# An fp32 encoder kernel: one of four remainders of the up projection's weights by a negated copy and an adding transfer

## The chip, the cores and the metric

The kernel runs on one core of one Trainium2 chip. The metric is device time in microseconds of one launch. A core has five engines that run their own instruction queues in order and meet at semaphores: TensorE (PE in the profile, with its weight loads as PEld), VectorE (DVE), ScalarE (ACT), GpSimd (POOL) and SyncE (SP). Transfers are issued from a queue of SP, ACT or POOL and carried out by 16 DMA engines.

## The reference

Two layers of a bidirectional encoder on 256 tokens of width 2048, in float32:

```python
for l in range(DEPTH):                       # 2
    h = rms_norm(x, ln1_g[l])
    proj = h @ w_in[l]                       # 2048 x 4608
    ...                                      # two groups of 8 heads: neighbourhood attention, windowed GQA
    x = x + o @ w_out[l]
    h2 = rms_norm(x, ln2_g[l])
    u = depthwise_conv(h2 @ w_up[l], conv_w[l], conv_b[l])     # 2048 x 11264, width 3 over positions
    gate, up = u[..., :D_FF], u[..., D_FF:]                    # D_FF = 5632
    x = x + (jax.nn.silu(gate) * up) @ w_down[l]
```

## The kernel before

**Products in parts.** The large products are computed in a reduced float32 format (F32R). To keep the accuracy, each factor is split in two parts: a high part, which is a copy rounded to F32R, and a remainder, the value minus the high part. Three products (high x high, high x remainder, remainder x high) are summed. `split` does it: ScalarE writes the high part (line 112), VectorE subtracts (line 113). For weights the tiles are `raw` (as loaded), `whi` and `wlo`.

**Quanta and half blocks.** All weights stream through the core once, in quanta of 1 MB (`raw`, 128 x 2048 floats, 3 buffers), loaded by SP's queue (line 742). A quantum is split and used in two halves of 128 x 1024 (three parts for the kind "seven"). A list `steps` of (quantum, half) sets the order; at step s the program first calls `split_w(s + SPLIT_AHEAD)` with SPLIT_AHEAD = 4, and then the products of step s. When the last half of a quantum has been split, the load of the quantum three further on is issued into its buffer. `whi` and `wlo` have five buffers each, so the split for step s + 4 waits until PE has finished step s - 1.

**The stages of a layer.** Input projection with attention around it, output projection, and then the feed-forward part. There, an *up block* is one 128-wide slice of gate and up columns: two quanta, four half blocks. After each block ScalarE evacuates PSUM (line 546), VectorE adds and scales (547, 548), POOL fills the halo of the convolution with two tiny copies (550, 551), ScalarE and VectorE do the convolution and the gate (556 to 562). The 44 up blocks come in runs of 9, 8, 8, 8 and 8, and three more that alternate with sevens. Between the runs stand quanta of the down projection: "plain", "seven" (one level of a scheme with seven products, whose raw weights VectorE combines first, lines 748 to 750) and "down".

**What sets the order.** The program is written in the order of `steps`; a scheduler places each instruction on its engine's queue by a simulated timeline and by priorities: a block under `tc.high_priority(offset=AHEAD_PRIO)` goes 40 places ahead. Tiles named `v_a` and `v_b` are the values of attention's two groups, 128 x 1024 floats each; in the feed-forward part nothing uses them.

Of the kernel before, what the change touches and what calls it, by code (L numbers as in the profile page):

```python
# [11 lines left out]
F32 = mybir.dt.float32  # L12
F32R = mybir.dt.float32r
I32 = mybir.dt.int32
AF = mybir.ActivationFunctionType
ALU = mybir.AluOpType
AX = mybir.AxisListType

P = 128
L = 2  # L20
T = 256
TT = T // P
# [18 lines left out]
NB = 4  # L41
# [8 lines left out]
AHEAD_PRIO = 40  # L50
# [3 lines left out]
WARM = 14  # L54

SPARE = 3 * (("qT", 3),)


@with_exitstack
def encoder_kernel(  # L60
# [5 lines left out]
    nc = tc.nc  # L66
    const = ctx.enter_context(tc.tile_pool(name="const", bufs=1))
    wp = ctx.enter_context(tc.tile_pool(name="wp", bufs=2))
    act = ctx.enter_context(tc.tile_pool(name="act", bufs=1))
# [27 lines left out]
    def mm(ps, lhsT, rhs, start, stop):  # L97
        nc.tensor.matmul(ps, lhsT, rhs, start=start, stop=stop, skip_group_check=True)  # L98

    def rsqrt(ps, inv_n, dst, tag):  # L100

        v = work.tile(list(dst.shape), F32, name="v_" + tag, bufs=1)
        nc.vector.tensor_scalar(v, ps, inv_n, EPS, op0=ALU.mult, op1=ALU.add)
        e = power[:, 0:math.prod(dst.shape[1:])]
        if len(dst.shape) == 3:
            e = e.rearrange("p (t h) -> p t h", t=TT)
        nc.gpsimd.tensor_tensor(dst, v, e, op=ALU.pow)
# [19 lines left out]
    st = {}  # L127
# [6 lines left out]
    def square_x(nb):  # L134
        if nb == 0:

            st["ss"] = act.tile([P, TT, NB + 24], F32, name="ss_x")[:, :, 0:NB]
        for tt in range(TT):
            sq = work.tile([P, TT, T], F32, name="prob", bufs=2)
            nc.scalar.activation(sq.rearrange("p t n -> p (t n)"), x[:, tt, nb * 512:(nb + 1) * 512], AF.Square,  # L140
                                 accum_out=st["ss"][:, tt, nb:nb + 1])
# [26 lines left out]
    def stat_o(grp):  # L168
        ps = psum.tile([P, TT], F32, name="pv", bufs=1)
        for tt in range(TT):  # L170
            mm(ps[:, tt:tt + 1], acc_o[grp][:, tt * P:(tt + 1) * P], ones[:, 0:1], True, True)
        st["ro"] = act.tile([P, TT], F32, name="ro", bufs=2)
        rsqrt(ps, 1.0 / (NH * HD), st["ro"], "c2")


# [229 lines left out]
    quanta = []  # L405
# [113 lines left out]
    def middle(l, f):  # L519

        name, bufs = "mid", MIDS
        if f >= NF - CHUNKS[-1]:
            k = count[l] = count.get(l, 0) + 1
            if k > MIDS:
                name, bufs = SPARE[k - MIDS - 1]
        return act.tile([P, 2, T], F32R, name=name, bufs=bufs)

    def q_up(l, f, u):
        def body(q, half, hi, lo):
            if u == 0 and half == 0:  # L530
                cur["up"] = psum.tile([P, 2, 2, T], F32, name="mm", bufs=2)
            ps = cur["up"]
            hv, lv = (w.rearrange("p (k j n) -> p k j n", k=4, j=2) for w in (hi, lo))
            for j in range(2):
                for kk in range(4):
                    k = 8 * u + 4 * half + kk
                    two(ps[:, j], hv[:, kk, j], lv[:, kk, j], xs[k], k == 0, k == KD - 1)
            if u == 1 and half == 1:
                glu(l, f, ps)
        return body  # L540
# [28 lines left out]
    ms, ss = {}, {}  # L569
# [15 lines left out]
    def q_seven(l, c, i):  # L585

        f = sum(CHUNKS[:c]) + 2 * i
        p = f // 2
        a, b = slice(0, P), slice(P, T)

        def body(q, part, hi, lo):
            if i == 0 and part == 0:
                t = psum.tile([P, 2, 512], F32, name="mm", bufs=2)
                ps = {1: t[:, 0], 6: t[:, 1]}
                for n, name, k in ((5, "S", 2), (7, "S", 2), (3, "tr", 1), (4, "pv", 1)):
                    ps[n] = psum.tile([P, 512], F32, name=name, bufs=k)
                cur["seven"] = ps
            ps = cur["seven"]
            hv, lv = (w.rearrange("p (k n) -> p k n", k=2) for w in (hi, lo))
            todo = (((3, ss[p, 3]), (1, gs[f][:, :, a])),  # L600
                    ((7, ss[p, 2]), (5, ss[p, 0])),
                    ((4, gs[f + 1][:, :, b]), (6, ss[p, 1])))[part]
            for j, (n, x2) in enumerate(todo):
                for x_part, w in ((0, hv), (1, hv), (0, lv)):
                    mm(ps[n], x2[:, x_part], w[:, j], i == 0 and x_part == 0 and w is hv,
                       i == PAIRS - 1 and w is lv)
            if i == PAIRS - 1 and part == 2:
                with tc.high_priority(offset=AHEAD_PRIO):
                    add_seven(ps)
        return body  # L610
# [89 lines left out]
    for l in range(L):  # L700
# [8 lines left out]
        for c, nf in enumerate(CHUNKS):  # L709
            up = lambda f: [(a["w_up"][l, f, u], q_up(l, f, u), "up") for u in range(2)]  # L710
            down = lambda nb, g: [(a["w_down"][l, sum(CHUNKS[:c]) // FG + g, nb], q_down(l, c, nb, g), "")]
            seven = lambda i: [(a["w_seven"][l, c, i], q_seven(l, c, i), "seven")]
# [17 lines left out]
                    quanta += down(nb, g)  # L730


    steps = [(q, h) for q in range(len(quanta)) for h in range(3 if quanta[q][2] == "seven" else 2)]
    raw, hl, left, loads, highs = {}, {}, {}, {}, {}

# [8 lines left out]
    def split_seven(w, part, hi, lo):  # L744

        hv, lv = (t.rearrange("p (k n) -> p k n", k=2) for t in (hi, lo))
        if part == 1:
            nc.vector.tensor_sub(w[:, 1:3], w[:, 1:3], w[:, 2:4])
            nc.vector.tensor_add(w[:, 3], w[:, 3], w[:, 1])
            nc.vector.tensor_sub(w[:, 0], w[:, 3], w[:, 0])  # L750
        return split(hv, lv, (w[:, 1::2], w[:, 1:3], w[:, 0::3])[part])

    def split_w(s, parts=1):
        if s < len(steps):
            q, half = steps[s]
            kind = quanta[q][2]
            o = UP_AT if kind == "up" else 0
            hl[s] = tuple(wp.tile([P, 1024 + 64], F32R, name=t, bufs=SPLIT_AHEAD + 1)[:, o:o + 1024]
                          for t in ("whi", "wlo"))
            with tc.high_priority(offset=AHEAD_PRIO if s >= KD // 2 else 0):  # L760
                if kind == "seven":
                    highs[s] = split_seven(raw[q].rearrange("p (k n) -> p k n", k=4), half, *hl[s])
                else:
                    m = 1024 // parts
                    for j in range(parts):
                        highs[s] = split(*(t[:, j * m:(j + 1) * m] for t in hl[s]),
                                         raw[q][:, half * 1024 + j * m:half * 1024 + (j + 1) * m])
            left[q] -= 1
            if left[q] == 0:
                del raw[q]  # L770
                load(q + LOAD_AHEAD)
# [15 lines left out]
    def first_x(i):  # L787
        for j in range(2):
            prep_x(0, 0, 2 * i + j, xT[i][:, j, :])
# [64 lines left out]
    for s, (q, half) in enumerate(steps):  # L854
        if s + SPLIT_AHEAD < KD // 2:
            first_x(s + SPLIT_AHEAD)
        split_w(s + SPLIT_AHEAD)
        quanta[q][1](q, half, *hl.pop(s))
        for f, args in side.pop((q, half), []):
            f(*args)  # L860
# [101 lines left out]
```

## Time and profile before

| what | value |
|---|---|
| time, median of 3 runs | 2090.1 us (2090.08 to 2090.17) |
| profiled execution: span, first to last instruction | 2088.2 us |
| granted TensorE clock | 1.000 |
| DVE, ACT, POOL busy | 82%, 59%, 8% of the span |
| DMA engines | mean 196 GB/s; 405 MB on SP's queue |
| splits of weights | 797 on ACT (1.057 us mean), 797 on DVE (1.221 us mean) |
| loads of 1 MB | 4.9 us from issue to landing (median) |

The profiled execution's own time is its span; the runs' median is 1.9 us above it, which lies around the span. In a group's row stand line, engine, operation, output <- input, shapes, count, then busy time and mean ns of one, then the idle time of the engine just before them and what ended most of it. In the list of waits stand engine, line, what ended the wait, then total us, times and the longest. A timeline row begins with start and duration in us.

### The profile page before, as it was taken

The page shows a single profiled execution, that of the slowest core. Times are in us where ns is not written, and L with a number is a line of the kernel's source. Part 1 is how long each engine was busy: PE and PEld are TensorE (multiplying, and loading weights), DVE is VectorE, ACT ScalarE, POOL GpSimd, SP SyncE. Part 2 cuts the span into 40 slices and gives each one's busy share as a digit, 9 for nine tenths or more (in the row PEclk, how much of TensorE's full clock was granted, in tenths as well). Part 3 has the DMA queues.
Part 4 walks back from the last instruction along what each step waited for, and adds up shares of the span by engine and source line. Part 5 has one row for each costly group of instructions (what it writes and reads, how often), then busy time and mean ns, then how long its engine had stood idle before and what let it go on. Part 6 is the DMA issues. An engine that isn't in the chain of part 4 may idle for free.

```text
span 2088.2 us, 29195 instructions
## 1 busy us (share of the span) xinstructions
PE 2082.8 (100%) x10816; PEld 1788.6 (86%) x10816; DVE 1719.4 (82%) x2604; ACT 1222.1 (59%) x1817; POOL 175.4 (8%) x237
## 2 busy tenths in 40 slices
PE   9999999999999999999999999999999999999999
PEld 8888888888888888888888888888888888888887
DVE  7786657898898988989757766578989989899896
ACT  7566556555555556556555665565656565555553
POOL 0011100100101001011000111001001010010100
PEclk9999999999999999999999999999999999999999
DMA  9544555556565564656655445555565655656554
GB/s 353 196 144 168 176 179 173 194 200 207 179 242 184 209 211 165 240 194 210 208 182 182 162 166 171 169 180 195 208 202 175 235 195 204 204 187 232 184 200 161
DMA packets 62143, 408.41 MB, mean 196 GB/s; under 512 B 7344, under 2 KB 9904, under 8 KB 13744
## 3 DMA queue, kind: packets, MB, share of 16 engines
q1 hardware_dynamic: 61280, 405.46, 56.4%
q8 instruction: 85, 1.39, 0.3%
q10 hardware_dynamic: 720, 1.08, 0.2%
q14 instruction: 58, 0.48, 0.1%
HBM read 404.42 MB, written 2.10 MB: 195 GB/s over the span
## 4 chain that ended last, share of the span: by engine, by line
PE 100%; ACT 0%; DVE 0%; issue 0%
PE mm L98 90%; PE S L98 4%; PE pv L98 3%; PE tr L98 2%; PE tr L373 1%; PE tr L307 1%; PE S L149 1%; ACT v_a L263 0%; ACT mid L115 0%; DVE x L689 0%; DVE ones L90 0%; DVE halfpi L94 0%; DVE power L92 0%
## 5 line engine op out<-in xcount | busy, mean ns | idle before, releaser
L112 ACT ACTIVATE whi<-raw 128x1024 fp32r<-128x1024 f32 (+1 forms) x797 | 830.8, 1057 | 684.3 <-PE mm L98 403.0
L113 DVE TENSOR_TENSOR wlo<-raw,whi 128x1024 fp32r<-128x1024 f32 (+1 forms) x797 | 964.8, 1221 | 271.9 <-ACT whi L112 234.6
L98 PE MATMUL mm<-xs,whi 128*128 128x512 f32 x2816 | 977.0, 390 | 0.0
L98 PE MATMUL mm<-xs,wlo 128*128 128x256 f32 x2816 | 794.1, 282 | 0.0
L98 PEld LDWEIGHTS mm<-xs,whi 128*128 128x128 f32 x2816 | 528.3, 188 | 110.5
L98 PEld LDWEIGHTS mm<-xs,wlo 128*128 128x128 f32 x2816 | 532.2, 189 | 1.1
L98 PE MATMUL mm<-whi,mid 128*128 128x512 f32 x1412 | 369.4, 391 | 0.4 <-ACT v_a L263 0.4
L98 PEld LDWEIGHTS mm<-whi,mid 128*128 128x128 f32 x1412 | 262.6, 188 | 54.5 <-ACT v_a L263 0.9
L98 PE MATMUL mm<-whi,xs 128*128 128x512 f32 x1152 | 294.7, 393 | 0.1
L98 PEld LDWEIGHTS mm<-whi,xs 128*128 128x128 f32 x1152 | 212.7, 188 | 42.6 <-ACT whi L112 0.8
L98 PE MATMUL mm<-wlo,mid 128*128 128x512 f32 x706 | 201.8, 391 | 0.0
L98 PE MATMUL mm<-wlo,xs 128*128 128x512 f32 x576 | 158.8, 392 | 0.0
L98 PEld LDWEIGHTS mm<-wlo,mid 128*128 128x128 f32 x706 | 132.2, 188 | 27.2
L558 DVE SCALAR_TENSOR_TENSOR pT<-halo,conv,pT 128x256 f32<-128x256 f32 x352 | 148.3, 480 | 0.9
L550 POOL COPY halo<-halo 128x6 f32<-128x6 f32 x88 | 40.6, 461 | 1233.6 <-DVE halo L548 1233.6
L98 PEld LDWEIGHTS mm<-wlo,xs 128*128 128x128 f32 x576 | 107.0, 188 | 21.4
L556 ACT ACTIVATE pT<-halo,conv 128x256 f32<-128x256 f32 x176 | 95.1, 588 | 5.8 <-DVE halo L548 5.7
L551 POOL COPY halo<-halo 128x6 f32<-128x6 f32 x88 | 76.0, 864 | 0.2 <-POOL halo L550 0.2
L548 DVE TENSOR_TENSOR halo<-prob,acc_b 128x512 f32<-128x512 f32 x88 | 60.7, 690 | 1.9
L547 DVE TENSOR_TENSOR prob<-prob,mm 128x512 f32<-128x512 f32 x88 | 60.0, 681 | 0.0
L546 ACT ACTIVATE prob<-mm 128x512 f32<-128x512 f32 x88 | 51.4, 584 | 7.1 <-PE mm L98 7.1
L560 ACT ACTIVATE prob<-pT 128x256 f32<-128x256 f32 x88 | 35.6, 404 | 30.3 <-DVE pT L558 30.3
(180 smaller groups left out, 1479.8 us busy)
## 6 DMA issues: line engine op xcount, KB each, us to landing
raw<-in_w_up SPq DMA_DIRECT2D x176, 1024.0 KB, 4.9
raw<-in_w_in SPq DMA_DIRECT2D x71, 1024.0 KB, 4.9
raw<-in_w_down SPq DMA_DIRECT2D x48, 1024.0 KB, 4.9
raw<-in_w_seven SPq DMA_DIRECT2D x40, 1024.0 KB, 4.9
raw<-in_w_out SPq DMA_DIRECT2D x32, 1024.0 KB, 4.8
raw<-in_w_plain SPq DMA_DIRECT2D x10, 1024.0 KB, 4.8
bias<-in_bias SPq DMA_DIRECT2D x16, 160.0 KB, 3.1
x<-in_x SPq DMA_DIRECT2D x4, 512.0 KB, 10.0
```

The costliest lines, as they stand in the source:

```text
L98: nc.tensor.matmul(ps, lhsT, rhs, start=start, stop=stop, skip_group_check=True)
L112: high = nc.scalar.activation(hi, src, AF.Copy)
L113: nc.vector.tensor_sub(lo, src, hi.bitcast(F32))
L149: nc.tensor.transpose(ps[:, j, tt * P:(tt + 1) * P], x[:, tt, (k + j) * P:(k + j + 1) * P], ident)
L546: nc.scalar.activation(t, ps[:, :, 0], AF.Copy)
L547: nc.vector.tensor_add(t, t, ps[:, :, 1])
L548: nc.vector.tensor_mul(ux[:, :, r:r + T], t, st["r2"][:, None, :].to_broadcast([P, 2, T]))
L550: nc.gpsimd.tensor_copy(ux[:, :, 1:r], ux[:, :, T:T + r - 1])
L551: nc.gpsimd.tensor_copy(ux[:, :, T + r:T + 2 * r - 1], ux[:, :, r + 1:2 * r])
L556: nc.scalar.activation(y[:, j, :], ux[:, j, r:r + T], AF.Identity, scale=w1, bias=b)
L558: nc.vector.scalar_tensor_tensor(y[:, j, :], ux[:, j, o:o + T], w, y[:, j, :], op0=ALU.mult, op1=ALU.add)
L560: nc.scalar.activation(t[:, 0, :], y[:, 0, :], AF.Silu)
```

## The change

For the last of the four half blocks of every up block (88 in all) the remainder is no longer a subtraction on VectorE. ScalarE writes the negated, rounded copy of `raw` into a tile, and a transfer issued on POOL's queue adds `raw` to it. This starts seven steps ahead instead of four, while the high part of that half is still copied at four. The remainders lie in `v_a` and `v_b` in turn. Two other tiles change their size by some bytes.

```diff
+EARLY = 7
...
-            st["ss"] = act.tile([P, TT, NB + 24], F32, name="ss_x")[:, :, 0:NB]
+            st["ss"] = act.tile([P, TT, NB + 20], F32, name="ss_x")[:, :, 0:NB]
...
-        st["ro"] = act.tile([P, TT], F32, name="ro", bufs=2)
+        st["ro"] = act.tile([P, 16], F32, name="ro", bufs=2)[:, 0:TT]
...
+    last_up, ups = {}, 0
+    for q in range(len(quanta)):
+        if quanta[q][2] == "up":
+            ups += 1
+            last_up[q] = ups % 2 == 0
...
+    lows = {}
+    turns = [0]
+
+    def by_transfer(s):
+        q, half = steps[s]
+        return quanta[q][2] == "up" and half == 1 and last_up[q]
+
+    def low_w(s):
+
+        if s < len(steps) and by_transfer(s):
+            q, half = steps[s]
+            src = raw[q][:, half * 1024:(half + 1) * 1024]
+            lo = lows[s] = act.tile([P, 1024], F32R, name=("v_a", "v_b")[turns[0] % 2], bufs=1)
+            turns[0] += 1
+            with tc.high_priority(offset=AHEAD_PRIO):
+                nc.scalar.activation(lo, src, AF.Copy, scale=-1.0)
+                nc.gpsimd.dma_start(out=lo, in_=src, accum_op=ALU.add)
+
     def split_w(s, parts=1):
...
+            early = lows.pop(s, None)
             hl[s] = tuple(wp.tile([P, 1024 + 64], F32R, name=t, bufs=SPLIT_AHEAD + 1)[:, o:o + 1024]
-                          for t in ("whi", "wlo"))
+                          if t == "whi" or early is None else early for t in ("whi", "wlo"))
             with tc.high_priority(offset=AHEAD_PRIO if s >= KD // 2 else 0):
-                if kind == "seven":
+                if early is not None:
+                    highs[s] = nc.scalar.activation(hl[s][0], raw[q][:, half * 1024:(half + 1) * 1024], AF.Copy)
+                elif kind == "seven":
...
+        low_w(s + EARLY)
         split_w(s + SPLIT_AHEAD)
```

In the changed kernel the lines lie further down: 546 is 548, 550 is 552, 619 is 621, the split's lines 112 and 113 are 114 and 115; the negated copy is line 775, the transfer 776, the high copy of that half 788.

Three places show what the change does to the order on the engines. The first is ACT's queue at the head of the third run of up blocks of layer 0, where the run of sevens ends (L619, later L621, belongs to the last seven; the rows behind it are the splits of the first two up blocks). The names in brackets are the semaphores waited for: DMAHW a load, DMASW a transfer of POOL's queue. Before:

```order
L112 ACTIVATE whi<-raw 128x1024 [waits DVE_49,PE_49]
L619 ACTIVATE tq<-mm 128x512 [waits DVE_49]
L112 ACTIVATE whi<-raw 128x1024 [waits DMAHW0_49,Activation_49]
L112 ACTIVATE whi<-raw 128x1024 [waits Activation_49]
L112 ACTIVATE whi<-raw 128x1024 [waits DMAHW1_49,PE_49,Activation_49]
L112 ACTIVATE whi<-raw 128x1024 [waits PE_49,Activation_49]
```

And now:

```order
L114 ACTIVATE whi<-raw 128x1024 [waits DVE_49,PE_49]
L621 ACTIVATE tq<-mm 128x512 [waits DVE_49]
L775 ACTIVATE v_b<-raw 128x1024 [waits DMAHW0_49,DMASW7_49]
L114 ACTIVATE whi<-raw 128x1024 [waits Activation_49]
L788 ACTIVATE whi<-raw 128x1024 [waits Activation_49]
L114 ACTIVATE whi<-raw 128x1024 [waits DMAHW1_49,PE_49,Activation_49]
L114 ACTIVATE whi<-raw 128x1024 [waits PE_49,Activation_49]
L775 ACTIVATE v_a<-raw 128x1024 [waits DMAHW2_49,DMASW0_49]
```

The negated copy of the first block stands just ahead of that quantum's two high copies, since all three wait for the same load; in the middle of a run it stands three splits ahead.

The second is ACT's queue where the three last up blocks of layer 0 alternate with sevens, from the split of the first seven's first part on (the row with DMAHW2). Before:

```order
L112 ACTIVATE whi<-raw 128x1024 [waits DMAHW2_49,PE_49,Activation_49]
L560 ACTIVATE prob<-pT 128x256 [waits DVE_49]
L112 ACTIVATE mid<-bias 128x256 [waits DVE_49]
L112 ACTIVATE whi<-raw 128x1024 [waits DVE_49,PE_49,Activation_49]
L546 ACTIVATE prob<-mm 128x512 [waits PE_49,Activation_49]
L112 ACTIVATE mid<-tq 128x256 [waits DVE_49]
L112 ACTIVATE whi<-raw 128x1024 [waits DVE_49,Activation_49]
L112 ACTIVATE whi<-raw 128x1024 [waits DMAHW3_49,PE_49,Activation_49]
```

And now:

```order
L114 ACTIVATE whi<-raw 128x1024 [waits DMAHW2_49,PE_49,Activation_49]
L562 ACTIVATE prob<-pT 128x256 [waits DVE_49]
L114 ACTIVATE mid<-bias 128x256 [waits DVE_49]
L775 ACTIVATE v_b<-raw 128x1024 [waits DMAHW4_49,DMASW7_49]
L114 ACTIVATE whi<-raw 128x1024 [waits DVE_49,PE_49,Activation_49]
L548 ACTIVATE prob<-mm 128x512 [waits PE_49,Activation_49]
L114 ACTIVATE mid<-tq 128x256 [waits DVE_49]
L114 ACTIVATE whi<-raw 128x1024 [waits DVE_49,Activation_49]
```

The negated copy for the up block behind that seven stands ahead of the seven's second split and of the evacuation of the block before, and waits for a later load (DMAHW4) than the split of the block's first half does (DMAHW3, one row further down).

The third is POOL's queue at the head of a run. Before, only the halo copies of one block after another stood there:

```order
L551 COPY halo_110<-halo_110 128x2x3 [waits Pool_49]
L550 COPY halo_112<-halo_112 128x2x3 [waits DVE_49,Pool_49]
L551 COPY halo_112<-halo_112 128x2x3 [waits Pool_49]
L550 COPY halo_110<-halo_110 128x2x3 [waits DVE_49,Pool_49]
```

And now:

```order
L553 COPY halo_110<-halo_110 128x2x3 [waits Pool_49]
L776 DMA v_b<-raw 128x1024 [waits DMASW7_49,DMAHW0_49,PE_49,Activation_49]
L776 DMA v_a<-raw 128x1024 [waits DMASW0_49,DMAHW2_49,PE_49,Activation_49]
L552 COPY halo_112<-halo_112 128x2x3 [waits DVE_49,Pool_49]
L553 COPY halo_112<-halo_112 128x2x3 [waits Pool_49]
L776 DMA v_b<-raw 128x1024 [waits DMASW1_49,DMAHW4_49,PE_49,Activation_49]
```

The halo copies of a block stand behind the transfers of the next one or two blocks, each of which waits for ACT's negated copy.

## The prediction

> **What bounds the kernel now.** I read the head of the page first (busy shares, the chain that ended last), then the list of waits of the tensor engine, then the windows of one run of up blocks, then the timeline around the places that the change touches.
>
> ```profile
> span 2088.2 us, 29195 instructions
> PE 2082.8 (100%) x10816; PEld 1788.6 (86%) x10816; DVE 1719.4 (82%) x2604; ACT 1222.1 (59%) x1817; POOL 175.4 (8%) x237
> PE 100%; ACT 0%; DVE 0%; issue 0%
> 600.00:688.70 88.70, 88.70 (x513) 78.62 (x512) 77.09 (x119) 50.60 (x73) 8.39 (x14) 1.00 0.59 201
> 596.00:612.00 16.00, 16.00 (x88) 13.93 (x87) 15.61 (x18) 7.64 (x8) 0.00 (x0) 1.00 0.81 291
> ```
>
> The columns of a window row are its length, then busy time of PE, PEld, DVE, ACT and POOL, the granted clock, the DMA share and GB/s. In the eight up blocks from 600.0 to 688.7 PE is busy all 88.7 us at clock 1.00, so a block takes 88.7 / 8 = 11.09 us and a half block 2.77 us. DVE is busy 77.1 us of it (87%), ACT 50.6 (57%). At the head of that run (596 to 612) DVE has 0.39 us free in 16 and the DMA engines are at 0.81: the fullest place that the change touches.
>
> What PE waited for in the whole execution is four rows, of its weight loads:
>
> ```profile
> PEld pv L98 <- DVE halfpi L94: 1.1, 1, 1.1
> PEld mm L98 <- ACT v_a L263: 0.9, 2, 0.4
> PEld mm L98 <- ACT whi L112: 0.8, 2, 0.5
> PEld mm L98 <- DVE prob L547: 0.3, 1, 0.3
> ```
>
> That is 3.1 us together. A faster VectorE or ScalarE can win no more than that, 0.15% of the span, and the first 1.1 us stand in the start, which the change leaves as it is. So the question is only whether the change makes PE wait.
>
> How far ahead of PE the splits run shows on one half block: its remainder (the DVE row) ends at 613.50, and PE starts on it at 622.19.
>
> ```profile
> 612.27 1.23 DVE L113 TENSOR_TENSOR wlo<-raw,whi 128x1024 fp32r<-128x1024 f32 x1 [0.47 <-ACT whi L112]
> 622.19 0.39 PE L98 MATMUL mm<-xs,whi 128*128 128x512 f32 x1
> ```
>
> The lead is 8.7 us in the middle of a run. It is the cover for everything that I cost at nothing below.
>
> **The change, part by part.**
>
> ```profile
> L112 ACT ACTIVATE whi<-raw 128x1024 fp32r<-128x1024 f32 (+1 forms) x797 | 830.8, 1057 | 684.3 <-PE mm L98 403.0
> L113 DVE TENSOR_TENSOR wlo<-raw,whi 128x1024 fp32r<-128x1024 f32 (+1 forms) x797 | 964.8, 1221 | 271.9 <-ACT whi L112 234.6
> L546 ACT ACTIVATE prob<-mm 128x512 f32<-128x512 f32 x88 | 51.4, 584 | 7.1 <-PE mm L98 7.1
> ```
>
> Removed: 88 subtractions on DVE of 1.221 us, 107 us of DVE time. Added: 88 negated copies on ACT. They have the shape of the hi copies, so 1.057 us each, 93 us: ACT goes from 50.6 to 59.1 us in the run of eight, 67%, and keeps 29 us free. Neither sum is on the path: gain 0, cost 0 under the 8.7 us of lead. Two tile sizes move by some bytes; no duration in the rows depends on them, and I price that at 0.
>
> Added: 88 transfers on the POOL queue, 512 KB read from raw, 512 KB read from the tile and 512 KB written. No row shows a transfer that adds. The nearest rows, from issue to landing:
>
> ```profile
> out<-x SPq DMA_DIRECT2D x6, 256.0 KB, 2.3
> raw<-in_w_up SPq DMA_DIRECT2D x176, 1024.0 KB, 4.9
> x<-in_x SPq DMA_DIRECT2D x4, 512.0 KB, 10.0
> q1 hardware_dynamic: 61280, 405.46, 56.4%
> ```
>
> Bounds: 2.3 us, a lighter transfer, and 10.0 us, the same 512 KB while other loads fill the engines. I take 7 us: the 4.9 of a load, which reads the same number of bytes as the transfer's two sources, plus about 2 because it shares the engines with a load in flight. The q1 row gives the engines' work: 0.564 x 2088.2 us for 405.46 MB, or 3.05 us per load. Two loads a block are 6.1 us of 11.09; the transfer adds 1.5 (if only the written bytes count) to 3.0 us (if both sources do), 69% to 82%. The Trainium skill's page "Collectives: The Full Stack", section "The bandwidth ceiling: the fold count and why AG ≠ RS ≠ AR", says that an adding DMA is limited by its two source reads and not by the addition. By that rule the sum is the upper one, 82%, still under the ceiling; no run here shows it yet.
>
> *In the middle of a run* the copy stands on ACT right behind the first split of the next block and ahead of the evacuation L546 of the block just done. It needs its load landed:
>
> ```profile
> 919.87 0.33 SPq L742 DMA_DIRECT2D raw<-in_w_up  x1
> 925.83 1.06 ACT L112 ACTIVATE whi<-raw 128x1024 fp32r<-128x1024 f32 x1 [0.78 <-ACT mid L112]
> 926.79 0.58 ACT L546 ACTIVATE prob<-mm 128x512 f32<-128x512 f32 x1
> ```
>
> The load issued at 919.87 has landed at 924.8; ACT is free for the copy at 926.8: 2.0 us in hand. Behind it wait L546, two further hi copies, and on DVE the rest of the block's gate work, each later by 1.06 us, against DVE's one subtraction less. PE needs the remainder 7 half blocks after the copy's place, 19.4 us, less 2.1 us for the two ACT copies: 17.3 us for a transfer of 7. Cost 0. The next load into the same raw slot now waits for the transfer instead of DVE; it stands behind the block's last hi copy, three half blocks (8.3 us) after the negated copy, when a transfer of 7 is done. On POOL the halo copies stand behind the transfer's issue, and DVE's gate work behind them; a delay there is inside the same lead.
>
> *At the head of the second to fifth run of up blocks of each layer* the lead is shorter, since the load is late there. The copy goes between L619 and the last two splits of the first block:
>
> ```profile
> 597.29 0.60 ACT L619 ACTIVATE tq<-mm 128x512 f32<-128x512 f32 x1 [1.78 <-DVE x L618]
> 597.84 2.01 ACT L112 ACTIVATE whi<-raw 128x1024 fp32r<-128x1024 f32 x2
> 608.32 0.39 PE L98 MATMUL mm<-xs,whi 128*128 128x512 f32 x1
> ```
>
> It ends at 597.84 + 1.06 = 598.9, and PE starts on this half block at 608.32: 9.4 us. With 7 us the cost is 0; with the bound of 10.0 it is 0.6 us x 8 places = 5 us; with 2.3 it is 0. This is the narrowest place.
>
> *Where sevens and up blocks alternate* (the last twelve of each layer), ACT's order now has the copy ahead of a split of the first seven and of L546, and it waits for a load issued at 942.05, so until 946.95.
>
> ```profile
> 942.05 0.33 SPq L742 DMA_DIRECT2D raw<-in_w_up  x1
> 946.38 1.06 ACT L112 ACTIVATE whi<-raw 128x1024 fp32r<-128x1024 f32 x1 [0.80 <-DVE raw L748]
> 948.14 0.60 ACT L546 ACTIVATE prob<-mm 128x512 f32<-128x512 f32 x1 [0.71 <-PE mm L98]
> 949.43 2.01 ACT L112 ACTIVATE whi<-raw 128x1024 fp32r<-128x1024 f32 x2 [0.39 <-DVE raw L750]
> 952.73 1.22 DVE L113 TENSOR_TENSOR wlo<-raw,whi 128x1024 fp32r<-128x1024 f32 x1
> 954.70 0.39 PE L98 MATMUL mm<-xs,whi 128*128 128x512 f32 x1
> ```
>
> The copy runs 946.95 to 948.0; the split moves from 946.38 to 948.0, L546 to 949.0, the pair of splits from 949.43 to about 950.0 after the idle 0.71 and 0.39 are used up. The remainder for the first up block there ends at 953.95 today and PE starts at 954.70, its first use of the remainder 0.23 later: 1.0 us of slack. A shift of 0.6 fits; a load later by 1 us from the transfers' traffic makes PE wait 0.6. Bounds 0 and 2 us; I take 0.5 us, twice: 1.0 us.
>
> Sum: 0 + 0 + 0 + 1.0 us. The profiled execution has a span of 2088.2; the runs' median is 2090.1, 1.9 us outside the span. Forecast 2090.1 + 1.0 = 2091.1 us: no change that a measurement of this kernel can tell (0.2% is 4.2 us).
>
> **Rivals.**
>
> *The transfer lands too late at the eight heads of runs (slower).* It decides from 9.4 us after the copy on. For it: the DMA share of 0.81 and the full DVE there, and this pair, in which a tiny POOL copy ends with DVE's subtraction:
>
> ```profile
> 800.14 1.23 DVE L113 TENSOR_TENSOR wlo<-raw,whi 128x1024 fp32r<-128x1024 f32 x1 [0.23 <-ACT whi L112]
> 800.16 1.25 POOL L551 COPY halo<-halo 128x6 f32<-128x6 f32 x1
> ```
>
> If POOL's work of issuing is held like that by two DVE instructions, 10.0 + 2 x 1.23 = 12.5 us, 3.1 us late, times 8: 25 us, 2115. Against it: the 4.9 us of a load. The Trainium skill's page "SBUF — State Buffer", section "Who interferes with whom", holds that a two-input DVE instruction blocks POOL's reads alone, and infers that issuing a transfer needs writes. By that rule the hold is 0; the pair agrees as far as the copy's read goes. Chance 0.24.
>
> *The transfers slow the loads until they pace the kernel (slower).* A copy waits for its load, and behind it come L546, the next hi copy, its subtraction and the load after next: T + 1.06 + 0.58 + 1.06 + 1.22 = T + 3.9 us against 11.09. From T = 7.2 us on each block loses; from T = 8.3 the 8.7 us of lead are gone within a run of eight. With T = 10.0 (the x row) it is 2.8 x 8 - 8.7 = 14 us per run, ten runs: 140 us, 2230. Against it: 4.9 + 3.0 = 7.9 us with the whole transfer in the way. Chance 0.10.
>
> *The relief of DVE pays (faster).* Even with all of the 3.1 us of waits gone it is 2087.0, inside the 0.2%. Only if matmuls themselves run quicker with other addresses would it be more, and no row hints at it. Chance 0.03.
>
> **Numbers.** No change 0.63, late at heads 0.24, loads 0.10, faster 0.03. Slower by over 0.2% is the two middle ones with a little of the first rival below 4.2 us given back: 0.33; faster 0.02; same 0.65. The range goes from 2088.0 (most of the 3.1 us won) to 2115 (the first rival's price); the second rival lies beyond.
>
> **What would show it.** Right: PE's wait list stays near 3 us; the L113 group has 709 entries and ACT 88 more; transfers take 5 to 9 us; no wait of PE on a transfer. Wrong: PE waiting for v_a or v_b at 608, or ACT's copy waiting for raw in every block with L546 drifting later through a run.

## The result, and the profile after

The changed kernel takes 2099.6 us (median of 4 runs, 2097.4 to 2101.0) against 2090.1 (2089.9 to 2090.2): 9.5 us or 0.45% slower, ratio 1.0045 with a 95% interval of 1.003 to 1.006. The forecast was 2091.1, with "no change" (0.65) as its likeliest case. The time lies in the range, in a case that was not the likeliest ("slower", 0.33). Two executions at a lower granted clock (2584 us at 0.752 in experiment 1, 2971 us at 0.654 in experiment 9) are left out of the medians below.

The head of the page of the changed kernel, VectorE's remainders, ScalarE's hi copies without a subtraction, and the transfers. In its lines `split` is L114 and L115, the load L749, the negated copy L775, the transfer L776, the hi copy L788, the evacuation of PSUM L548 and, on VectorE, L549:

```profile
span 2097.1 us, 29473 instructions
PE 2086.1 (99%) x10816; PEld 1787.8 (85%) x10816; DVE 1623.0 (77%) x2516; ACT 1308.8 (62%) x1905; POOL 241.5 (12%) x325
q0 software_dynamic: 12672, 46.14, 12.3%
...
L115 DVE TENSOR_TENSOR wlo<-raw,whi 128x1024 fp32r<-128x1024 f32 (+1 forms) x709 | 858.2, 1221 | 298.2 <-ACT whi L114 265.8
L788 ACT ACTIVATE whi<-raw 128x1024 fp32r<-128x1024 f32 x88 | 92.7, 1053 | 40.1 <-PE mm L100 40.1
...
raw<-in_w_up SPq DMA_DIRECT2D x176, 1024.0 KB, 5.7
v_a<-raw POOLq DMA_DIRECT2D x44, 512.0 KB, 5.5
v_b<-raw POOLq DMA_DIRECT2D x44, 512.0 KB, 5.1
```

The edit did what it says: 709 subtractions instead of 797, 96 us less on VectorE, 87 us more on ScalarE. A transfer takes 5.1 to 5.5 us, and the load of an up quantum 5.7 instead of 4.9. The DMA engines' work for a transfer is 0.123 x 2097.1 / 88 = 2.93 us.

PE's list of waits over the whole execution (total us, times, longest):

```profile
PEld mm L100 <- DVE prob L549: 5.9, 4, 2.2
PEld mm L100 <- DVE wlo L115: 1.5, 2, 0.8
PEld mm L100 <- ACT whi L114: 1.4, 3, 0.6
PEld pv L100 <- DVE halfpi L96: 1.1, 1, 1.1
PEld mm L100 <- ACT v_a L265: 0.9, 2, 0.4
PEld pv L100 <- ACT whi L114: 0.2, 1, 0.2
```

That is 11.0 us instead of 3.1, and none of it is a wait for a transfer. To see where, I followed the start of the n-th matmul (10816 in both) from the trace of before to that of after. The difference is 0.3 us after the first 20 us and 0.6 at 905. Then it steps up by 0.6 at 955, 2.0 at 986 and 1.0 at 1003, and in the second layer by 0.5, 1.5 and 0.8 at 2000, 2031 and 2047. These six places belong to the last three up blocks of each layer, which alternate with sevens; they make 6.4 of the 8.5 us at the end. Most of the rest comes in small steps between 1000 and 1060, in the second layer's attention and behind 2060.

The largest step, on ScalarE, SP and POOL. The first fence has ScalarE's rows of before, the second those of after (start, length in us, in brackets the idle time before and what ended it):

```profile
976.25 0.40 ACT L560 ACTIVATE prob<-pT 128x256 f32<-128x256 f32 x1
978.41 2.01 ACT L112 ACTIVATE whi<-raw 128x1024 fp32r<-128x1024 f32 x2 [1.76 <-PE mm L98]
980.33 0.40 ACT L112 ACTIVATE qT<-bias 128x256 fp32r<-128x256 f32 x1
981.13 1.06 ACT L112 ACTIVATE whi<-raw 128x1024 fp32r<-128x1024 f32 x1 [0.40 <-PE mm L98]
982.10 0.58 ACT L546 ACTIVATE prob<-mm 128x512 f32<-128x512 f32 x1
```

```profile
978.41 0.40 ACT L562 ACTIVATE prob<-pT 128x256 f32<-128x256 f32 x1
981.75 1.06 ACT L775 ACTIVATE v_b<-raw 128x1024 fp32r<-128x1024 f32 x1 [2.94 <-DMA raw<-in_w_up]
982.71 1.99 ACT L114 ACTIVATE whi<-raw 128x1024 fp32r<-128x1024 f32 x2
984.61 0.40 ACT L114 ACTIVATE qT<-bias 128x256 fp32r<-128x256 f32 x1
984.91 1.04 ACT L114 ACTIVATE whi<-raw 128x1024 fp32r<-128x1024 f32 x1
985.86 0.57 ACT L548 ACTIVATE prob<-mm 128x512 f32<-128x512 f32 x1
...
967.69 0.87 POOL L776 DMA_DIRECT2D v_a<-raw  x1 [13.21 <-ACT v_a L775]
...
988.27 0.50 PE L100 MATMUL mm<-xs,whi 128*128 128x512 f32 x1 [1.75 <-DVE prob L549]
```

PE could not start the third of the three blocks until L549 had emptied the PSUM of the second. L549 needs the evacuation L548, which came 3.8 us later than before (1.3 of it is the shift that PE's work already had). In ScalarE's queue L548 stands behind two splits of a seven in one row (I call them *the pair*), and the pair now stands behind the third block's negated copy, which waited for its load (the third block's second quantum; I call it *the late load*). What held that load shows SP's list of waits from 960 to 990 in the changed kernel:

```profile
SPq L749 <- DMA v_a<-raw: 6.9, 1, 6.9
```

It goes into the raw buffer from which the second block's transfer, issued at 967.69, still reads. SP's rows, before and after, each have two loads in one row, the late load the second of them:

```profile
968.29 3.80 SPq L742 DMA_DIRECT2D raw<-in_w_up  x2
```

```profile
969.56 7.71 SPq L749 DMA_DIRECT2D raw<-in_w_up  x2
```

So the late load left at 976.95 instead of 971.76 (a row's end less the 0.33 us of an issue) and landed at 981.7 instead of 977.1.

So the first theory was *held and blocked*: the transfer holds the raw buffer, the load comes late, and the copy blocks ScalarE's queue. Its rivals: *order alone* (the copy's place suffices), *hold alone* or *late loads alone*, *traffic* (the transfers slow the loads, whatever they hold), and *spread* (the other 82 transfers cost it).

### The profile page after: what moved, and what is told of

The parts are those of the page before. It is cut to its first block, busy times and chain, and to the rows that moved or that the text cites. A ratio compares the mean times of both kernels' runs of the same rounds, so it can differ in the third digit from the quotient of the medians.

```text
span 2097.1 us, 29473 instructions
## 1 busy us (share of the span) xinstructions
PE 2086.1 (99%) x10816; PEld 1787.8 (85%) x10816; DVE 1623.0 (77%) x2516; ACT 1308.8 (62%) x1905; POOL 241.5 (12%) x325
## 3 DMA queue, kind: packets, MB, share of 16 engines
q0 software_dynamic: 12672, 46.14, 12.3%
## 4 chain that ended last, share of the span: by engine, by line
PE 95%; DVE 2%; DMA 1%; issue 1%; ACT 1%; ACTq 0%; DVEq 0%; SPq 0%
PE mm L100 86%; PE S L100 3%; PE pv L100 2%; PE tr L100 1%; DVE wlo L115 1%; PE tr L375 1%; ACT whi L114 1%; PE tr L309 1%; PE S L151 0%; DMA v_a<-raw 0%; DMA mid<-in_xT 0%; DMA raw<-in_w_seven 0%; DMA raw<-in_w_up 0%; DVE pT L560 0%; DVE prob L549 0%
## 5 line engine op out<-in xcount | busy, mean ns | idle before, releaser
L115 DVE TENSOR_TENSOR wlo<-raw,whi 128x1024 fp32r<-128x1024 f32 (+1 forms) x709 | 858.2, 1221 | 298.2 <-ACT whi L114 265.8
L114 ACT ACTIVATE whi<-raw 128x1024 fp32r<-128x1024 f32 (+1 forms) x709 | 736.4, 1053 | 449.9 <-PE mm L100 220.7
L100 PE MATMUL mm<-xs,wlo 128*128 128x256 f32 x2112 | 596.4, 282 | 0.6 <-DVE wlo L115 0.6
L100 PEld LDWEIGHTS mm<-xs,wlo 128*128 128x128 f32 x2112 | 399.1, 189 | 2.6 <-DVE wlo L115 1.5
L552 POOL COPY halo<-halo 128x6 f32<-128x6 f32 x88 | 78.4, 891 | 352.8 <-DVE halo L550 352.8
L788 ACT ACTIVATE whi<-raw 128x1024 fp32r<-128x1024 f32 x88 | 92.7, 1053 | 40.1 <-PE mm L100 40.1
L100 PE MATMUL mm<-xs,v_a 128*128 128x256 f32 x352 | 99.3, 282 | 0.0
L100 PE MATMUL mm<-xs,v_b 128*128 128x256 f32 x352 | 99.2, 282 | 0.0
L776 POOL DMA_DIRECT2D v_b<-raw x44 | 38.1, 866 | 524.1 <-ACT v_b L775 299.6
L549 DVE TENSOR_TENSOR prob<-prob,mm 128x512 f32<-128x512 f32 x88 | 60.3, 685 | 46.9 <-ACT prob L548 46.9
```

Source lines behind the costliest of these rows:

```text
L114: high = nc.scalar.activation(hi, src, AF.Copy)
L115: nc.vector.tensor_sub(lo, src, hi.bitcast(F32))
L549: nc.vector.tensor_add(t, t, ps[:, :, 1])
L552: nc.gpsimd.tensor_copy(ux[:, :, 1:r], ux[:, :, T:T + r - 1])
L776: nc.gpsimd.dma_start(out=lo, in_=src, accum_op=ALU.add)
L788: highs[s] = nc.scalar.activation(hl[s][0], raw[q][:, half * 1024:(half + 1) * 1024], AF.Copy)
```

## The experiments

All are edits of the changed kernel except the first, and each was timed beside the kernel before (2090.1 in every comparison). "Alternating blocks" are the last three up blocks of each layer, six of 88; in the edits `alt[q]` is true for their quanta. A kernel was profiled once, so a time inside it is that of one execution.

**1. The two tile sizes alone**, in the kernel before:

```diff
-st["ss"] = act.tile([P, TT, NB + 24], ...)
+st["ss"] = act.tile([P, TT, NB + 20], ...)
-st["ro"] = act.tile([P, TT], ...)
+st["ro"] = act.tile([P, 16], ...)[:, 0:TT]
```

> The kernel before with nothing but the two tile sizes of the change (ss smaller by 32 bytes per partition, ro larger). Theory addresses (the later tiles lie at other addresses, and products that read mid and qT take 231 to 235 ns instead of 227, as they do at 1010 us in every variant so far): 2091.0 to 2092.0 us, a step of 0.6 to 0.7 us between 1000 and 1060 us. Rival (that slowing comes from the transfers or from the order of the products): 2090.1 us, 227 ns.

Measured: 2091.8 us, 1.7 above before, as the theory has it. The ratio's interval, 0.9999 to 1.0017, just includes 1, but each of the 11 executions (2091.7 to 2092.5) lies above each of the 28 of before (2089.9 to 2091.2). The n-th matmul is 0.66 us later after the stretch from 1000 to 1060 and 0.3 more behind 2060, as in the changed kernel. PE's groups from 1011 to 1022, before and with the sizes (count, then busy us and mean ns):

```profile
L98 PE MATMUL mm<-whi,qT 128*128 128x512 f32 x24 | 7.2, 389 | 0.0
L98 PE MATMUL mm<-whi,mid 128*128 128x512 f32 x8 | 3.1, 389 | 0.0
```

```profile
L98 PE MATMUL mm<-whi,qT 128*128 128x512 f32 x24 | 7.4, 395 | 0.0
L98 PE MATMUL mm<-whi,mid 128*128 128x512 f32 x8 | 3.2, 395 | 0.0
```

Products of the same shape and number take 6 ns more, without a wait. In the layout qT (and v_a, v_b) begin 32 bytes lower, mid, whi and wlo where they were. So the two sizes, which I had priced at 0, cost about 1.7 us, by where tiles lie and not by any wait. How is open: the products of mid and whi, neither of which moved, are slower too in this stretch, where they alternate with those of qT.

**2. No transfer in the alternating blocks**, 82 of 88 left:

```diff
-            last_up[q] = ups % 2 == 0
+            last_up[q] = ups % 2 == 0 and not (ups - 1) // 2 % NF >= sum(CHUNKS[:-1]) + PART + 1
```

The right side of the comparison is 41, of 44 up blocks.

> The last three up blocks of each layer (those that alternate with sevens) keep the old split, so 82 of 88 transfers stay. Theory (held and blocked: there the transfer holds its raw buffer, the load after next starts about 5 us late, and the next negated copy, waiting for that load, stands ahead of a seven's splits and the PSUM evacuation): 2090 to 2091 us, PE waits of 3 us, and the shift of the matmuls against before stays under 0.5 us everywhere. Rivals order alone, hold alone and traffic in the alternation: the same, 2090 to 2091. Rival spread (the 82 other transfers or the time around the span cost part of the 9.5 us): 2093 to 2099.

Measured: 2092.4 us (ratio 1.0013, 1.0004 to 1.0023). The six steps are gone, and with them 7.2 of the 9.5 us. The time lies between the two forecasts. Against experiment 1 the 82 transfers cost 0.6 us: spread is wrong as the main cause. The 2.3 us that remain are the tile sizes and this 0.6. In PE's list stands now

```profile
PEld mm L100 <- DMA v_a<-raw: 0.3, 1, 0.3
```

one head of a run where the transfer came 0.3 us late.

**3. The copy without its transfer** in the alternating blocks; the copy is read by nobody, VectorE subtracts:

```diff
-                nc.gpsimd.dma_start(out=lo, in_=src, accum_op=ALU.add)
+                if not alt[q]:
+                    nc.gpsimd.dma_start(out=lo, in_=src, accum_op=ALU.add)
...
+            if early is not None and alt[q]:
+                early = None
```

> The last three up blocks of each layer make the negated copy at the same place but issue no transfer; the copy is read by nobody, and the remainder is subtracted on VectorE as before. Theory held and blocked: 2090.5 to 2092 us: without the transfer the load after next starts on time (about 972, not 977), the copies find their loads landed, and only the first copy's wait (0.6 us per layer) may stay. Rival order alone (the copy ahead of split and evacuation is enough): 2097 to 2099.5. Rival hold alone: 2090 to 2091. Rival traffic: 2090 to 2091.

Measured: 2095.0 us (1.0022, 1.0013 to 1.0032), 2.6 more than experiment 2. Held and blocked allowed 2092 at most, hold alone and traffic 2091, order alone 2097 at least: all miss. The copies alone cost a part; the late load left at 974.1 and landed at 979.35, 2.2 us later than before (1.5 of it shift) with no transfer near it. PE does not wait at 986 there; it waits 0.4 at 955, 0.35 at 970 and 1.1 at 2010.

**4. The transfer reads memory, not raw**, in the alternating blocks; ScalarE's order and the bytes stay, raw is not held:

```diff
-                nc.gpsimd.dma_start(out=lo, in_=src, accum_op=ALU.add)
+                wide = quanta[q][0][:, half * 1024:(half + 1) * 1024]
+                nc.gpsimd.dma_start(out=lo, in_=wide if alt[q] else src, accum_op=ALU.add)
```

> In the last three up blocks of each layer the adding transfer reads the weights from memory a second time instead of from the raw buffer; ScalarE's order is that of the changed kernel, the bytes of the transfer stay, and the raw buffer is no longer held by it. Theory held and blocked: 2090.5 to 2093 us, the load of the third block's second quantum starts near 972. Rival order alone: 2097 to 2099.5. Rival hold alone: 2090 to 2092. Rival traffic (512 KB more in flight slow the loads, whatever they read): 2098 to 2100, the loads take as long as with the transfer from raw.

Measured: 2099.8 us (1.0046, 1.0031 to 1.0061), as the changed kernel. The hold is not needed. The chain that ended last has the late load, which now leaves on time (971.15) and takes nearly twice as long (9.64 us; before 5.4); and in the window from 971.5 to 973.5 the queues' shares of the engines are:

```profile
971.15 9.64 DMA raw<-in_w_up
```

```profile
q0 software_dynamic: 77, 0.32, 89.1%
q1 hardware_dynamic: 6, 0.02, 3.0%
```

In these 2 us the loads (q1) all but stand still beside the transfer (q0). It is not so for the whole of a transfer: over all of this one, 971.1 to 976.8, the shares are 51.8% and 44.6%, and in the changed kernel at the same place, from 971 to 976:

```profile
q0 software_dynamic: 141, 0.52, 55.5%
q1 hardware_dynamic: 126, 0.92, 45.5%
```

The engines have little room there: all queues together have 0.95 of them from 969.5 to 971 and 0.97 from 971.1 to 976.8 in this run. So held and blocked is wrong in its first half: whether the load waits for the buffer or for the engines, it lands some 4 us late (981.7 held, 980.8 not; 1.3 and 0.9 of it are shift). *Traffic* had forecast this time (2098 to 2100), *order alone* 2099.5 at most; the 9.64 us speak for traffic. The Trainium skill's page "DMA: Bandwidth & Descriptors", section "Queues, rings and completion order", says that each engine takes turns between queues by whole packets, typically of 9 to 17 descriptors. A transfer leaves 12672 / 88 = 144 records, 9 for each of 16 engines, so by that rule an engine may finish its share before it turns to a load; the 3.0% agree with that, the 44.6% and 45.5% over a whole transfer do not, and no run varied it.

The next theory was *pushed and blocked*: the transfer pushes the loads back, and the copy that waits for its load blocks ScalarE's queue.

**5. The copy late**: behind the hi copy of the half block before, so behind what it had blocked.

```diff
-            with tc.high_priority(offset=AHEAD_PRIO):
+            with tc.high_priority(offset=AHEAD_PRIO), (tc.issue_after(highs[s - 1].ins) if late else nullcontext()):
                 nc.scalar.activation(lo, src, AF.Copy, scale=-1.0)
...
-        low_w(s + EARLY)
+        low_w(s + EARLY, False)
+        low_w(s + 4, True)
```

`late` is true for the alternating blocks, which the second call makes.

> In the last three up blocks of each layer the negated copy is put behind the hi copy of the half block before, so behind the PSUM evacuation; the transfer reads raw as in the changed kernel and ends later than there. Theory held and blocked: 2090 to 2093 us: the loads stay late or get later (after 977 for the one of the third block), but nothing stands behind the copy. Rival order alone: 2090 to 2091. Rival hold alone (late loads pace PE): 2099 or more. Rival traffic: 2099.

Measured: 2101.7 us (1.0051, 1.0034 to 1.0068). Two of SP's waits from 960 to 990, and PE's largest over the whole execution:

```profile
SPq L750 <- DMA v_a<-raw: 10.1, 1, 10.1
SPq L750 <- DMA v_b<-raw: 8.5, 1, 8.5
...
PEld mm L100 <- DVE prob L549: 6.3, 2, 3.4
```

The hold is longer, and PE still waits for the evacuation: at 970 L548 stands behind the second block's own split, whose load lands at 969.8. A late load blocks ScalarE without any copy ahead of it. Held and blocked, 2093 at most, misses; hold alone and traffic had forecast 2099 or more. Part of this time is something else. The two waits are 2.9 and 3.4 us long (start to start of two matmuls, 970.21 and 2016.01), and behind each PE's granted clock was halved. This profile is of the slowest of its four executions (2102.9). The windows behind the first (length, PE, PEld, DVE, ACT, POOL, clock, DMA share, GB/s):

```profile
974.40:977.40 3.00, 3.00 (x11) 2.55 (x10) 3.00 (x5) 0.80 (x2) 0.00 (x0) 0.50 0.74 146
977.40:980.00 2.60, 2.60 (x17) 2.28 (x16) 2.60 (x6) 1.36 (x2) 0.00 (x0) 1.00 0.32 43
```

From 970.0 to 974.4 the clock is 0.96, so the half clock lasted some 3.0 + 0.4 us and cost about 1.7 us more than the wait. In the changed kernel's trace, whose longest interval is 2.1 us, the clock stays at 1.00.

**6. Late copy and transfer from memory**, 4 and 5 together.

> In the last three up blocks of each layer the copy stands behind the half block before, as in the run with the late copy (2101.7), and the transfer reads memory a second time, so raw is free early. Theory pushed and blocked: 2092 to 2095 us (the late copy waits for nothing, and the loads come 3 us late at most instead of 6). Rival late loads alone: 2097 to 2100. Rival order alone: 2092.4, and then the run with the late copy stays unexplained.

Measured: 2100.4 us (1.0050, 1.0037 to 1.0063). That is above every forecast, and it does not decide between them, because a new wait took the place of the old one:

```profile
PEld mm L100 <- DMA v_b<-in_w_up: 7.1, 4, 2.2
PEld mm L100 <- ACT whi L114: 2.1, 4, 1.2
```

Issued at 956.65, the transfer lands 10.4 us later, 2 us after PE needed it. Here it is the remainder itself that is late.

**7. The transfer without ScalarE's copy**: GpSimd clears the tile, the transfer adds raw as soon as it has landed, and VectorE subtracts as before.

```diff
-                nc.scalar.activation(lo, src, AF.Copy, scale=-1.0)
+                if alt[q]:
+                    nc.gpsimd.memset(lo.bitcast(F32), 0.0)
+                else:
+                    nc.scalar.activation(lo, src, AF.Copy, scale=-1.0)
...
+            if early is not None and alt[q]:
+                early = None
```

> In the last three up blocks of each layer GpSimd clears the tile, the transfer adds raw to it as soon as the load has landed, nobody reads it, and the remainder is subtracted on VectorE as before: the transfer's traffic and its hold on raw stay, ScalarE's copy is gone. Theory pushed and blocked (the transfer pushes the loads back by 3 to 5 us, and only the copy that waits for its load ahead of a split and of the evacuation turns that into waits of PE): 2092 to 2094.5 us, although the load of the third block's second quantum is late. Rival late loads alone make PE wait: 2097 to 2100. Rival order alone: 2092.4, as without transfers and copies there.

Measured: 2093.9 us (1.0020, 1.0011 to 1.0029), 1.5 above experiment 2. The profile is of the slowest of its ten executions (2097.1); 3.0 us of that come between 1824 and 1880, away from the alternating blocks. The transfer starts 2 us earlier here (965.76), the late load lands at 980.2, and PE waits 0.7 at 986 behind the same evacuation, with ScalarE in its old order. It comes by another way, VectorE's preparation of the seven (L758 in this kernel), whose own load was in flight with the transfer and landed at 973.4 instead of 970.8:

```profile
981.03 2.01 ACT L114 ACTIVATE whi<-raw 128x1024 fp32r<-128x1024 f32 x2 [1.77 <-DVE raw L758]
...
984.20 0.58 ACT L548 ACTIVATE prob<-mm 128x512 f32<-128x512 f32 x1
```

So traffic makes PE wait without the copy, but by less than the rival's price. The time is the one of pushed and blocked; the wait is not, since that theory had none without the copy. Copies and transfers are not two separate prices: the transfers add 1.5 us to no copies and 4.6 to the copies.

**8. Half a transfer**: the copy as in the changed kernel, the transfer on 512 of 1024 columns, VectorE on the others.

```diff
-                nc.gpsimd.dma_start(out=lo, in_=src, accum_op=ALU.add)
+                n = 512 if alt[q] else 1024
+                nc.gpsimd.dma_start(out=lo[:, 0:n], in_=src[:, 0:n], accum_op=ALU.add)
...
+                    if alt[q]:
+                        nc.vector.tensor_sub(early[:, 512:1024], src[:, 512:1024], hl[s][0][:, 512:1024].bitcast(F32))
```

> In the last three up blocks of each layer the copy is made in full and at the same place, but the transfer adds only half of the columns; VectorE subtracts the others. Theory pushed and blocked: between the copy without transfer (2095.0) and the changed kernel (2099.6), 2096 to 2098.5, since the engines' time of a transfer is halved. Rival order alone: 2095 or less. Rival hold alone (any transfer holds raw until it lands, mostly latency): 2098.5 to 2100.

Measured: 2095.0 us (1.0023, 1.0014 to 1.0032), the same as the copy with no transfer. The forecast of an even dose (2096 to 2098.5) misses: half the transfer costs nothing in the median, the other half 4.6 us. What the price goes by is a threshold, and the profiles show it at one place. "The pair" is when the two splits of the seven started, less the shift that PE's work had already at 976; "PE waits" is the step between 980 and 996 (starts of the n-th matmul against before, in the first layer). The profile of 8 is its slowest execution (2096.1), and 5 and 6 are not in the table, since they have no pair behind a copy:

| run | start, shift | the pair | behind what | PE waits |
|---|---|---|---|---|
| before | 978.4, 0 | 978.4 | PE | 0 |
| none there (2) | 978.7, 0.4 | 978.3 | PE | 0 |
| first and third only (10) | 979.1, 1.1 | 978.0 | the copy | 0 |
| copy alone (3) | 980.6, 1.5 | 979.1 | the copy, VectorE | 0 |
| half a transfer (8) | 980.8, 0.9 | 979.9 | the copy, late load | 0.5 |
| transfer alone (7) | 981.0, 0.9 | 980.1 | VectorE, the seven's load | 0.7 |
| second only (9) | 981.2, 0.8 | 980.5 | VectorE, the seven's load | 1.1 |
| transfer from memory (4) | 981.8, 0.9 | 981.0 | the copy, late load | 1.6 |
| changed kernel | 982.7, 1.3 | 981.4 | the copy, late load | 2.0 |
| changed, old sizes (11) | 982.3, 0.7 | 981.6 | the copy, late load | 2.2 |

Up to 979.1 nothing happens, and the waits lie on a line from 979.4 on: PE waits one us for each us (2.0 at 981.4, 0.5 at 979.9), whatever made the pair late. The second layer has the same line with its edge at 2019.6 (0.8 at 2020.3 in experiment 7, 1.5 at 2021.1 in the changed kernel, 1.8 at 2021.4 in experiment 4). The kernel before stands about 1 us from the edge in each layer (978.4 and 2018.65).

**9 and 10. One block of three, two blocks of three.** In 9 only the second alternating block keeps copy and transfer, in 10 only the first and third:

```diff
-            last_up[q] = ups % 2 == 0
+            last_up[q] = ups % 2 == 0 and (ups - 1) // 2 % NF - sum(CHUNKS[:-1]) - PART - 1 not in (0, 2)
```

```diff
-            last_up[q] = ups % 2 == 0
+            last_up[q] = ups % 2 == 0 and (ups - 1) // 2 % NF - sum(CHUNKS[:-1]) - PART - 1 != 1
```

The number compared is 0, 1 or 2 for the three alternating blocks of a layer.

> Of the last three up blocks of each layer only the second keeps copy and transfer. Theory late load (the second block's transfer makes the load of the third block's second quantum land 3 to 5 us late; PE then waits about one us for each us by which it lands after 978.4, counted without the shift so far, as the runs so far have it: 0.5 at 978.8, 0.7 at 979.3, 1.6 at 979.9, 2.0 at 980.4): 2094.5 to 2098 us, no wait of PE at 955, a wait of 1 to 2 us near 986 and 2031, and those near 1003 and 2047 only as far as they follow from it. Rival order alone (the copy): 2093.3, a third of the copies' 2.5 us. Rival third block (its own transfer is the dear one): 2093.

> Of the last three up blocks of each layer the first and the third keep copy and transfer, the second is split as before. Theory late load: that load lands by 978.4, so nothing near 986 and 2031; 0.5 us stays near 955 and 2000, and up to 1 us near 1003 and 2047 by the third's own transfer: 2093 to 2095.5 us. Rival order alone: 2094.1, two thirds of 2.5 us. Rival third block: 2097 or more.

Measured: 2095.0 us (1.0024, 1.0014 to 1.0033) and 2093.5 (1.0017, 1.0007 to 1.0027). Both times are as the late load has it, and so are the places in the first layer, but in 9 not the way: the late load lands at 978.9 without the shift, for which that theory had 0.5 us, and the pair stands behind VectorE and the seven's load (landed at 973.6), as in experiment 7. The second block's copy and transfer alone make the waits at 986 (1.1) and 2031 (1.1), and one of 0.6 at 2014, with no copy of the third block in ScalarE's queue; without it PE does not wait at either place nor at 1003, only 0.4 at 2047. Together they cost 2.6 + 1.1 = 3.7 us above experiment 2, all three 7.2: with the first block's copy ahead of it the second block's copy comes at 966.24 instead of 964.37, its transfer ends later, and the load behind it too.

**11. The changed kernel with the old tile sizes**, all transfers kept (experiment 1 backwards):

> The changed kernel with the two tile sizes of before, all transfers kept; v_a and v_b then start 32 bytes higher, as in the kernel before. Theory addresses: the matmuls near 1010 us take 227 ns again and the time falls by 1.7 us, to 2097.9 (2097 to 2099). Rival (the sizes were there for the transfers, which are slower into the old places): the transfers take longer than 5.1 to 5.5 us, and the time is 2099.6 or more.

Measured: 2095.6 us (1.0029, 1.0017 to 1.0041; six runs from 2094.8 to 2099.0). The transfers take 5.4 and 5.1 us, as long as with the new sizes, so the rival falls. The time fell by 4.0 us and not by 1.7, more than the theory allowed (2097 at least). The products at 1011 are back at their old rate (about 1 us of it by the shifts), and the steps in the alternating blocks are 4.7 us instead of 6.4, mostly in the second layer, where the late load leaves 2.4 us earlier. Why it does is not settled; the times of this kernel and of the changed one (2097.4 to 2101.0) overlap.

**12. The old sizes and no transfer in the alternating blocks**, 2 and 11 together:

> The changed kernel without the six copies and transfers of the last three up blocks of each layer and with the two tile sizes of before; 82 of 88 transfers stay. If what was found adds up: 2092.4 - 1.7 = 2090.7 us (2090.2 to 2091.4), the same as before within 0.2%, with about 100 us less work of VectorE. Rival (the 82 transfers cost more once the addresses are right): 2092 or more.

Measured: 2090.8 us (1.0004, 0.9995 to 1.0013): no change against before, and none better. The 82 transfers cost 0.7 us and win nothing, since PE has nothing to win. PE waits 0.5 us for a transfer at one head of a run in this profile.

## Why the prediction was right or wrong

**What bounds it: right.** Relieving VectorE of 96 us won nothing in any run.

**The middle of runs: right, 0.** From 600.0 to 688.7 the changed kernel's window shows PE without a gap, VectorE down by 8.5 us, ScalarE up by 8.4, the DMA engines at the 0.82 that was the upper sum: 27.2% for the transfers and 54.8% for the loads. The Trainium skill's page "Collectives: The Full Stack", section "The bandwidth ceiling: the fold count and why AG ≠ RS ≠ AR", states the rule of two source reads, there for ReduceScatter; by it a transfer was estimated at 3.0 us of engine time, and the trace has 2.93. The window:

```profile
600.00:688.70 88.70, 88.70 (x513) 78.54 (x512) 68.56 (x109) 59.03 (x82) 15.36 (x22) 1.00 0.82 250
```

**The heads of runs: the cost of 0 was right, by a hair.** I took 7 us for the transfer against a lead of 9.4. The narrowest place of the changed kernel is not the first block of a run, as I had it, but the third of one: the copy starts at 878.77, the transfer is issued at 880.23, and PE is at its result at 890.51 (ScalarE's, POOL's and PE's rows, and the transfer in the list of DMA issues from 878 to 892):

```profile
878.77 1.06 ACT L775 ACTIVATE v_b<-raw 128x1024 fp32r<-128x1024 f32 x1 [1.52 <-DMA raw<-in_w_up]
880.23 0.86 POOL L776 DMA_DIRECT2D v_b<-raw  x1 [0.53 <-ACT v_b L775]
890.51 0.28 PE L100 MATMUL mm<-xs,v_b 128*128 128x256 f32 x1
```

```profile
v_b<-raw POOLq DMA_DIRECT2D x1, 512.0 KB, 10.0
```

10.0 us of 10.3: the upper bound of my price was the true one where loads are in flight (the longest of the 88 took 10.5), and the median of 5.1 to 5.5 says nothing of it. That no head paid is luck. The first rival's place was nearly right, its price not: the first three blocks of the runs cost 0 here, and at one place each 0.3 to 0.7 us in experiments 2, 3, 8, 10 and 12. That POOL's issuing is held by VectorE no run shows; the 0.87 us that an issue takes here leave no room for the 2 x 1.23 of that rival.

**The alternating blocks: the step that failed.** I gave 0.5 us for each layer, bounds 0 and 2, and measured is 3.6 and 2.8 (the six steps). I followed only the first of three blocks, and the copy's own wait there; its step of 0.6 and 0.5 is what I had allowed for. I did not ask when the loads *beside and behind* a transfer land. For the middle of a run I had argued that the next load into the slot comes three half blocks after the copy. In the alternating part the slot is asked for 4.5 us after the copy's start (966.24 to 970.7), and in the kernel before three loads leave within 6 us (966.0 to 971.8), so the 2.93 us of the transfer come on top of engines that were at 0.89 there before (966 to 976). The second rival's chain, a late load ahead of the evacuation on ScalarE, was the right mechanism; I had looked for it in the long runs, where it does not occur. And my slack of 1.0 us was that of the first block's remainder; the 1.0 us that decided is the pair's. That the measured time still lies in the range is luck too: the upper end, 2115, was the price of the heads, which cost nothing.

**The two tile sizes: mis-sized.** Priced at 0 because no duration in the rows depended on them; 1.7 us alone.

In medians: tile sizes 1.7, the 82 transfers with their copies 0.6, the six copies 2.6, the six transfers on top of them 4.6, together 9.5. The parts are not independent (experiments 7, 9, 10 and 11).

**The signs.** The 709, the 88, PE without a wait on a transfer, and the 5 to 9 us came out, the last with exceptions (4.5 to 10.5; 9.3 from issue to SP's release in the alternating part). PE's list did not stay near 3 us, and neither of the two signs that I had named for "wrong" was the one that came.

## What to carry to other kernels

Cost a transfer not only by its own deadline but by what lands after it: find the next loads on the same engines and the next use of the buffer that it reads, and follow them to the instruction that stands first in an in-order queue. Do this at the place where loads leave closest together, not in the steady state; the six of 88 transfers there cost, with their copies, more than ten times what the other 82 did (7.2 and 0.6 us). A change of a tile's size moves the tiles behind it, so time it alone before reading the rest.

## What the runs showed of the hardware

Beside an adding transfer from GpSimd's queue the loads of SyncE's queue got 3.0% of the engines against 89.1% for 2 us of experiment 4, and 45.5% against 55.5% from 971 to 976 in the changed kernel; what decides between the two is open. The same 512 KB take 5.1 to 5.5 us in the median and up to 10.5. Matmuls of one shape took 395 instead of 389 ns when two tile sizes changed and qT began 32 bytes lower, those of mid and whi, which had not moved, among them; which of the two sizes or tiles does it was not tried. A wait of PE of 2.9 us was followed by some 3.4 us at a granted clock of 0.50, one of 2.1 us in another trace was not. The Trainium skill's page "TensorE: Matmul & The Clock Gate", section "Part 1: The HAM clock gate (the "warmup" mystery)", gives an idle window of about 3.4 us for that; here the shorter wait was enough.
